# A jump past TensorE's program and back, ahead of its work, in a masked-prefix-sum and matmul kernel

## The chip, the cores and the metric

One core of a Trainium2 chip runs the kernel. The metric is the device time of one execution, in microseconds (us). For each version the median of several executions is given; a profile is one further execution, recorded by the hardware profiler.

## The reference

```python
B, S, D = 8, 8192, 512          # x: B x S x D f32, lengths: B int64, w: D x D f32
mask = (pos < lengths[:, None, None])
cs = np.cumsum(x * mask, axis=1)
midpoints = (lengths // 2).clip(0)
mid_features = cs[b_idx, midpoints, :]
return np.matmul(mid_features[:, None, :], w).squeeze(1)
```

Only one row of each running sum is used. So for each of the 8 batches the kernel adds up the first n = min(lengths // 2 + 1, lengths) rows of x, and multiplies the 8 sums by w. With the lengths of this draw n is 570, 2690, 256, 2057, 905, 3772, 3859 and 571: 14,680 rows of 2 KB.

## The kernel before

The sums are made on TensorE: a matmul of 0/1 weights (128 rows of x by 8 batches) with 128 rows of x adds those rows up into `s_ps` in PSUM, at the row of the batch that they belong to. Four such matmuls, for the four groups `j` of a tile, go to four bands of columns of the array and write four bands of `s_ps`; the bands are added at the end.

The rows of a batch come in whole blocks of 512 rows (1 MB, the tile `xt`, with 8 block slots for each of two buffers `q`) and a remainder of under 512 rows (the tile `rem`, in four pieces). The first block of batch 0 has a tile of its own, `first`, and is loaded without knowing the lengths. Batches are handled in pairs: a loop of four passes whose body holds batch `q=0` and batch `q=1`. How many blocks a batch has is known only at run time. Each engine that needs it reads the lengths into registers (the class `Counts`), and `whole_blocks` is a nest of eight branches, one for each block: the body of block k is entered if n has that many rows.

The program is written out by hand, engine by engine, with semaphores:

- SyncE (`block.sync`, line 166) issues the lengths, `first`, and the `xt` blocks, each once its slot is free (`s_free`, line 178), and at the end half of the output.
- ScalarE (`block.scalar`, line 193) issues w (line 154) ahead of everything, then the remainders, and at the end evicts and stores the other half.
- GpSimd clears `rem`. VectorE (line 259) builds the weights and, per batch, copies them to `cur` (line 322).
- TensorE (`block.tensor`, line 335) first clears `s_ps` (line 344, after VectorE's `zb`), broadcasts the row counts to all partitions (`n_ps`, line 347), reads the lengths into registers (lines 115 and 348), adds `first` (line 353), and enters the loop (line 354): wait for `cur` and `rem` (`take`, line 103), four matmuls on `rem`, then for each block a wait for its landing (again line 103) and four matmuls on `xt` (line 339), then a branch (line 145). After the loop come a small closing matmul (line 373), the sums' transposition by a `fold` matrix (line 379), and the product with w (line 387). An fp32 matmul is four instructions: a weight load and a matmul, twice.

A DMA adds 16 to its semaphore, one from each of the 16 DMA engines when its part has landed; `take(pe, s_full[q][k], 16)` therefore waits for the slowest of the sixteen.

[...]

Of the kernel before, what the change touches and what calls it, by code (L numbers as in the profile page):

```python
# [11 lines left out]
P = 128  # L12
# [3 lines left out]
def kernel(  # L16
# [17 lines left out]
    B, S, D = x.shape  # L34
    G = 4
    BLK = P * G
    NB = S // 2 // BLK
    KC = D // P
# [4 lines left out]
    PARTS = [(256, 0, 2, 4), (128, 1, 4, 4), (64, 3, 4, 2)]  # L43
# [6 lines left out]
    def sb(name, shape, dt=F32):  # L50
        return ctx.enter_context(nc.sbuf_tensor(name, shape, dt))

    def ps(name, shape):
        return ctx.enter_context(nc.psum_tensor(name, shape, F32))

    def sem(name):
        return tc.alloc_semaphore(name)

    xt = sb("xt", [P, 2, NB, G, D])
    first = sb("first", [P, G, D])  # L60
    rem = sb("rem", [P, 2, G, D])
    wt = sb("wt", [P, KC, D])
# [3 lines left out]
    n_f = sb("n_f", [1, B])  # L66
    ones = sb("ones", [1, P])
    zb = sb("zb", [1, 32], mybir.dt.bfloat16)
# [8 lines left out]
    first_w = sb("first_w", [P, B])  # L77
    table = sb("table", [P, B * (WT + 1)])
    cur = sb("cur", [P, 2, WT])
    zero = sb("zero", [1, D])  # L80
    fold_i = sb("fold_i", [P, B], I32)
    fold = sb("fold", [P, B])
    s_sb = sb("s_sb", [P, KC, P])
    mf_sb = sb("mf_sb", [P, KC, B])
    o_sb = [sb(f"o_sb{h}", [B, D // 2]) for h in range(2)]

    s_ps = ps("s_ps", [P, D])
    mf_ps = [ps(f"mf_ps{h}", [P, D]) for h in range(2)]
    o_ps = ps("o_ps", [P, D])
    n_ps = ps("n_ps", [P, D])  # L90

    s_full = [[sem(f"full{q}_{k}") for k in range(NB)] for q in range(2)]
    s_free = [[sem(f"free{q}_{k}") for k in range(NB)] for q in range(2)]
    s_rem = [sem(f"rem{q}") for q in range(2)]
    s_rfree = [sem(f"rfree{q}") for q in range(2)]
    s_cur = [sem(f"cur{q}") for q in range(2)]
    s_w, s_first, s_len1, s_go, s_out = sem("w"), sem("first"), sem("len1"), sem("go"), sem("out")
    s_pool, s_dve, s_pe = sem("pool"), sem("dve"), sem("pe")
    s_act = sem("act")

    def take(eng, s, n):

        eng.wait_ge(s, n).then_inc(s, -n)  # L103
# [39 lines left out]
    def whole_blocks(eng, n, body, k=0):  # L143
        if k < NB:
            with eng.If_cmp(n, BLK * (k + 1), "IS_GE"):
                body(k)
                whole_blocks(eng, n, body, k + 1)

    DVE_SEL, DVE_N, DVE_MASK = 2, 6, 28
# [16 lines left out]
    @block.sync  # L166
    def _(sp):
        ns = Counts(sp, s_len1, 16)
        sp.sem_inc(s_go, 1)
        base, at = sp.alloc_register("sp_base"), sp.alloc_register("sp_at")  # L170
        sp.reg_mov(base, 0)
        ns.without_first(base)
        with sp.Fori(0, B // 2):
            for q in range(2):
                n = ns.rows(q)

                def load_block(k):
                    take(sp, s_free[q][k], 1)
                    sp.dma_start(
                        out=xt[:, q, k],  # L180
                        in_=rows(sp, at, base, k * BLK, BLK).rearrange("(p g) d -> p g d", g=G),
                    ).then_inc(s_full[q][k], 16)

                whole_blocks(sp, n, load_block)

                sp.reg_alu(base, base, S, ALU.add)
                sp.reg_alu(base, base, ~(S - 1), ALU.bitwise_and)
            ns.next_pair()

        sp.wait_ge(s_dve, DVE_LAST)  # L190
        sp.dma_start(out=out[:, :D // 2], in_=o_sb[0][:]).then_inc(s_out, 16)
# [143 lines left out]
    @block.tensor  # L335
    def _(pe):
        def add(j, weights, rows):

            return pe.matmul(s_ps[32 * j:32 * j + B], lhsT=weights, rhs=rows,  # L339
                             start=False, stop=False, skip_group_check=True,  # L340
                             tile_position=(0, 32 * j))

        pe.wait_ge(s_dve, DVE_SEL)
        pe.matmul(s_ps[:], lhsT=zero[:, :P], rhs=zero[:], start=True, stop=False,  # L344
                  skip_group_check=True)
        pe.wait_ge(s_dve, DVE_N)
        pe.matmul(n_ps[:, :B], lhsT=ones[:], rhs=n_f[:], start=True, stop=True).then_inc(s_pe, 1)  # L347
        ns = Counts(pe, s_go, 1)
        ns.without_first()
        pe.wait_ge(s_dve, DVE_MASK)  # L350
        pe.wait_ge(s_first, 16)
        for j in range(G):
            add(j, first_w[:], first[:, j])
        with pe.Fori(0, B // 2):
            for q in range(2):
                take(pe, s_cur[q], 1)
                take(pe, s_rem[q], 16 * (len(PARTS) + 1))
                for j in range(G):
                    mm = add(j, cur[:, q, B + j * B:2 * B + j * B], rem[:, q, j])
                    if j == 0:  # L360
                        mm.then_inc(s_pe, 1)
                mm.then_inc(s_rfree[q], 1)

                def add_block(k):
                    take(pe, s_full[q][k], 16)
                    for j in range(G):
                        mm = add(j, cur[:, q, :B], xt[:, q, k, j])
                    mm.then_inc(s_free[q][k], 1)

                whole_blocks(pe, ns.rows(q), add_block)  # L370
            ns.next_pair()

        pe.matmul(s_ps[:32, :1], lhsT=zb[:], rhs=zb[:, :1], start=False, stop=True,  # L373
                  skip_group_check=True).then_inc(s_pe, 1)

        for h in range(2):
            pe.wait_ge(s_dve, DVE_MASK + 1 + h)
            for i in range(2):
                mm = pe.matmul(mf_ps[h][:, i * B:(i + 1) * B], lhsT=s_sb[:, 2 * h + i],  # L379
                               rhs=fold[:], start=True, stop=True)  # L380
            mm.then_inc(s_pe, 1)
        pe.wait_ge(s_w, 16)
        for kc in range(KC):
            if kc % 2 == 0:
                pe.wait_ge(s_dve, DVE_MASK + 3 + kc // 2)
            for j in range(4):
                mm = pe.matmul(o_ps[32 * j:32 * j + B, :P], lhsT=mf_sb[:, kc],  # L387
                               rhs=wt[:, kc, j * P:(j + 1) * P],
                               start=(kc == 0), stop=(kc == KC - 1), tile_position=(0, 32 * j))
            if kc % 2:  # L390
                mm.then_inc(s_pe, 1)

    block.__exit__(None, None, None)
    nc.sync.wait_ge(s_out, 32)
# [30 lines left out]
```

## Time and profile before

| | us |
|---|---|
| median of 5 executions (lowest, highest) | 89.78 (89.05, 92.21) |
| profiled execution, its own time | 90.06 |
| its span, first to last instruction | 87.9 |
| TensorE busy with matmuls / weight loads | 51.6 / 9.3 |
| VectorE, GpSimd, ScalarE busy | 8.1, 4.0, 2.0 |
| bytes moved by DMA | 31.28 MB, 356 GB/s over the span |
| mean clock granted to TensorE | 0.843 of full speed |

A row of the profile names the line, the engine and the tiles (out<-in). PE is TensorE's matmul side, PEld its weight loads, and a "q" after an engine's name is its instruction sequencer, which does waits, branches and DMA issues. DMA queue q1 is fed by SyncE and q10 by ScalarE. The rows of slices cut the span into 40 equal pieces; their digits are tenths.

### The profile page before, as it was taken

What the parts mean: (1) busy time and instruction counts of PE and PEld (TensorE: products, weight loads), DVE (VectorE), ACT (ScalarE), POOL (GpSimd) and SP (SyncE); (2) the same over time, 40 slices, a digit from 0 to 9 for tenths busy, and PEclk for the clock granted to TensorE, in tenths of its full rate; (3) what the DMA queues carried; (4) which work ended last, traced back from release to release, by engine and by line L of the source; (5) the groups of instructions that cost most, each with busy time, mean ns of one, the idle gap of its engine ahead of it and who ended that gap; (6) DMA issues with size and microseconds to landing.
All of it is one profiled execution on the core that took longest, in us unless ns stands there. A gap on an engine that the chain in (4) does not pass through costs nothing. (4 is left out here: it accounts for less than half of the span.)

```text
span 87.9 us, 1267 instructions
## 1 busy us (share of the span) xinstructions
PE 51.6 (59%) x317; PEld 9.3 (11%) x317; DVE 8.1 (9%) x42; ACT 2.0 (2%) x4; POOL 4.0 (5%) x9
## 2 busy tenths in 40 slices
PE   1801605996409795089944087754963487777720
PEld 1300000120001010001100000000210000010610
DVE  3685000000000000000000000000000000000520
ACT  0000000000000000000004200000000000000020
POOL 0970000000000000000000000000000000000000
PEclk9999999999995799755699855597599955599999
DMA  1899999999999999999999999999999999930000
GB/s 30 320 429 306 382 403 422 425 414 417 443 391 417 429 417 421 417 417 416 418 421 418 415 438 417 417 425 417 417 429 417 417 429 421 432 145 7 0 3 4
DMA packets 4693, 31.28 MB, mean 356 GB/s; under 512 B 658, under 2 KB 674, under 8 KB 946
## 3 DMA queue, kind: packets, MB, share of 16 engines
q1 hardware_dynamic: 3762, 27.27, 75.1%
q10 hardware_dynamic: 928, 3.97, 11.4%
q8 instruction: 1, 0.02, 0.1%
q14 instruction: 2, 0.02, 0.0%
HBM read 31.23 MB, written 0.02 MB: 355 GB/s over the span
## 5 line engine op out<-in xcount | busy, mean ns | idle before, releaser
L339 PE MATMUL s_ps<-xt,cur 128*8 128x512 f32 x200 | 34.5, 782 | 21.1 <-PEq L103 21.1
L339 PE MATMUL s_ps<-rem,cur 128*8 128x512 f32 x64 | 12.5, 866 | 4.9 <-PEq L103 4.7
L339 PEld LDWEIGHTS s_ps<-xt,cur 128*8 128x8 f32 x200 | 4.4, 92 | 49.3 <-issue 49.3
L322 DVE COPY cur<-table 128x40 f32<-128x40 f32 x8 | 1.4, 184 | 55.2 <-PE s_ps L339 55.2
L339 PE MATMUL s_ps<-first,first_w 128*8 128x512 f32 x8 | 1.9, 1040 | 4.3 <-DMA first<-in_x_dram 4.3
L257 POOL MEMSET rem<- 128x2048 f32 x2 | 3.5, 1805 | 0.0
L339 PEld LDWEIGHTS s_ps<-rem,cur 128*8 128x8 f32 x64 | 1.8, 98 | 16.6 <-issue 16.5
L344 PE MATMUL s_ps<-zero 1*128 1x512 f32 x2 | 2.1, 1136 | 1.8 <-DVE zb L268 1.8
L268 DVE COPY s_sb<-s_ps 128x256 f32<-128x256 f32 x2 | 0.8, 424 | 17.4 <-PE s_ps L373 17.4
L240 ACT ACT_TABLE_LOAD x1 | 1.3, 1283 | 47.4 <-issue 47.4
L379 PE MATMUL mf_ps<-fold,s_sb 128*128 128x8 f32 x8 | 1.1, 260 | 0.5 <-DVE s_sb L268 0.5
L243 ACT COPY o_sb<-o_ps 8x128 f32<-8x128 f32 x2 | 0.5, 259 | 35.4 <-PE o_ps L387 35.4
L387 PE MATMUL o_ps<-wt,mf_sb 128*8 128x128 f32 x32 | 1.1, 273 | 0.0
L379 PEld LDWEIGHTS mf_ps<-fold,s_sb 128*128 128x128 f32 x8 | 1.0, 190 | 0.6 <-DVE s_sb L268 0.6
L347 PEld LDWEIGHTS n_ps<-n_f,ones 1*128 1x128 f32 x2 | 0.7, 332 | 1.0 <-DVE n_f L268 0.5
L387 PEld LDWEIGHTS o_ps<-wt,mf_sb 128*8 128x8 f32 x32 | 0.8, 89 | 0.0
L344 PEld LDWEIGHTS s_ps<-zero 1*128 1x128 f32 x2 | 0.5, 305 | 1.8 <-DVE zb L268 1.8
L268 DVE COPY o_sb<-o_ps 8x128 f32<-8x128 f32 x2 | 0.6, 280 | 0.9 <-PE o_ps L387 0.8
L339 PEld LDWEIGHTS s_ps<-first,first_w 128*8 128x8 f32 x8 | 0.2, 90 | 4.4 <-DVE table L268 4.4
L268 DVE MEMSET zero<- 1x512 f32 x1 | 0.5, 485 | 1.1 <-SPq L48 1.1
L268 DVE TENSOR_SCALAR thr_i<-thr_i 128x2 int32<-128x2 int32 x1 | 0.5, 490 | 0.0
L347 PE MATMUL n_ps<-n_f,ones 1*128 1x8 f32 x2 | 0.4, 286 | 0.0
(36 smaller groups left out, 5.5 us busy)
## 6 DMA issues: line engine op xcount, KB each, us to landing
xt<-in_x_dram SPq DMA_DIRECT2D x25, 1024.0 KB, 15.5
rem<-in_x_dram ACTq DMA_DIRECT2D x3, 512.0 KB, 7.2
wt<-in_w_dram ACTq DMA_DIRECT2D x1, 1024.0 KB, 4.9
first<-in_x_dram SPq DMA_DIRECT2D x1, 1024.0 KB, 6.9
rem<-in_x_dram ACTq DMA_DIRECT2D x3, 256.0 KB, 6.5
rem<-in_x_dram ACTq DMA_DIRECT2D x3, 128.0 KB, 6.5
rem<-in_x_dram ACTq DMA_DIRECT2D x3, 32.0 KB, 5.5
rem<-in_x_dram ACTq DMA_DIRECT2D x1, 64.0 KB, 6.4
```

Of the source, the lines that this page charges most:

```text
L240: act.copy(out=warm[:], in_=zero[:, :1])
L243: copy = act.copy(out=o_sb[1][:, j * P:(j + 1) * P], in_=o_ps[64 + 32 * j:64 + 32 * j + B, :P])
L257: pool.memset(rem[:, q], 0.0).then_inc(s_rfree[q], 1)
L268: do(*args, **kw).then_inc(s_dve, 1)
L322: dve.tensor_copy(out=cur[:, b % 2], in_=table[:, b * WT:(b + 1) * WT]).then_inc(s_cur[b % 2], 1)
L339: return pe.matmul(s_ps[32 * j:32 * j + B], lhsT=weights, rhs=rows, start=False, stop=False, skip_group_check=True, tile_position=(0, 32 * j))
L344: pe.matmul(s_ps[:], lhsT=zero[:, :P], rhs=zero[:], start=True, stop=False, skip_group_check=True)
L347: pe.matmul(n_ps[:, :B], lhsT=ones[:], rhs=n_f[:], start=True, stop=True).then_inc(s_pe, 1)
L379: mm = pe.matmul(mf_ps[h][:, i * B:(i + 1) * B], lhsT=s_sb[:, 2 * h + i], rhs=fold[:], start=True, stop=True)
L387: mm = pe.matmul(o_ps[32 * j:32 * j + B, :P], lhsT=mf_sb[:, kc], rhs=wt[:, kc, j * P:(j + 1) * P], start=(kc == 0), stop=(kc == KC - 1), t ...
```

## The change

Everything that TensorE does is put into a loop of two passes, under a condition that holds in the second pass alone. In the first pass the branch of the condition leads from the start of the program to its end, and the loop's own branch leads back. The instructions inside are the same, in the same order. On TensorE a register move, two branches, a register step and the loop's closing branch come in; the other engines' instructions stay as they are. Lines from 344 on move down by three.

```diff
-        pe.wait_ge(s_dve, DVE_SEL)
-        pe.matmul(s_ps[:], lhsT=zero[:, :P], rhs=zero[:], start=True, stop=False,
-                  skip_group_check=True)
+
+        with pe.Fori(0, 2) as i:
+            with pe.If(i >= 1):
+                pe.wait_ge(s_dve, DVE_SEL)
+                pe.matmul(s_ps[:], lhsT=zero[:, :P], rhs=zero[:], start=True, stop=False,
+                          skip_group_check=True)
...
-        with pe.Fori(0, B // 2):
-            for q in range(2):
-                take(pe, s_cur[q], 1)
+                with pe.Fori(0, B // 2):
+                    for q in range(2):
+                        take(pe, s_cur[q], 1)
...
-        pe.wait_ge(s_w, 16)
-        for kc in range(KC):
-            if kc % 2 == 0:
-                pe.wait_ge(s_dve, DVE_MASK + 3 + kc // 2)
+                pe.wait_ge(s_w, 16)
+                for kc in range(KC):
+                    if kc % 2 == 0:
+                        pe.wait_ge(s_dve, DVE_MASK + 3 + kc // 2)
```

More of the change, by code (lines that the diff above doesn't have):

```diff
@@ L341, in add @@
                              tile_position=(0, 32 * j))
-        pe.wait_ge(s_dve, DVE_SEL)
-        pe.matmul(s_ps[:], lhsT=zero[:, :P], rhs=zero[:], start=True, stop=False,
-                  skip_group_check=True)
[L346 to L353, printed above, removed]
@@ L354, in _ @@
-        with pe.Fori(0, B // 2):
-            for q in range(2):
-                take(pe, s_cur[q], 1)
-                take(pe, s_rem[q], 16 * (len(PARTS) + 1))
-                for j in range(G):
-                    mm = add(j, cur[:, q, B + j * B:2 * B + j * B], rem[:, q, j])
-                    if j == 0:
-                        mm.then_inc(s_pe, 1)
[L362 to L381, printed above, removed]
-        pe.wait_ge(s_w, 16)
-        for kc in range(KC):
-            if kc % 2 == 0:
-                pe.wait_ge(s_dve, DVE_MASK + 3 + kc // 2)
[L386 to L391, printed above, removed]
+        with pe.Fori(0, 2) as i:
[3 more added lines that the diff above has]
+                          skip_group_check=True)
+                pe.wait_ge(s_dve, DVE_N)
+                pe.matmul(n_ps[:, :B], lhsT=ones[:], rhs=n_f[:], start=True, stop=True).then_inc(s_pe, 1)
+                ns = Counts(pe, s_go, 1)
+                ns.without_first()
+                pe.wait_ge(s_dve, DVE_MASK)
+                pe.wait_ge(s_first, 16)
+                for j in range(G):
+                    add(j, first_w[:], first[:, j])
+                with pe.Fori(0, B // 2):
+                    for q in range(2):
+                        take(pe, s_cur[q], 1)
+                        take(pe, s_rem[q], 16 * (len(PARTS) + 1))
+                        for j in range(G):
+                            mm = add(j, cur[:, q, B + j * B:2 * B + j * B], rem[:, q, j])
+                            if j == 0:
+                                mm.then_inc(s_pe, 1)
+                        mm.then_inc(s_rfree[q], 1)
+                        def add_block(k):
+                            take(pe, s_full[q][k], 16)
+                            for j in range(G):
+                                mm = add(j, cur[:, q, :B], xt[:, q, k, j])
+                            mm.then_inc(s_free[q][k], 1)
+                        whole_blocks(pe, ns.rows(q), add_block)
+                    ns.next_pair()
+                pe.matmul(s_ps[:32, :1], lhsT=zb[:], rhs=zb[:, :1], start=False, stop=True,
+                          skip_group_check=True).then_inc(s_pe, 1)
+                for h in range(2):
+                    pe.wait_ge(s_dve, DVE_MASK + 1 + h)
+                    for i in range(2):
+                        mm = pe.matmul(mf_ps[h][:, i * B:(i + 1) * B], lhsT=s_sb[:, 2 * h + i],
+                                       rhs=fold[:], start=True, stop=True)
+                    mm.then_inc(s_pe, 1)
+                pe.wait_ge(s_w, 16)
+                for kc in range(KC):
+                    if kc % 2 == 0:
+                        pe.wait_ge(s_dve, DVE_MASK + 3 + kc // 2)
+                    for j in range(4):
+                        mm = pe.matmul(o_ps[32 * j:32 * j + B, :P], lhsT=mf_sb[:, kc],
+                                       rhs=wt[:, kc, j * P:(j + 1) * P],
+                                       start=(kc == 0), stop=(kc == KC - 1), tile_position=(0, 32 * j))
+                    if kc % 2:
+                        mm.then_inc(s_pe, 1)
```

## The prediction

> **What bounds the kernel now.** I read the page's slices first, then its queues, then the stretches around the end, the order of time there, and last the queues again in short windows.
>
> ```profile
> DMA  1899999999999999999999999999999999930000
> q1 hardware_dynamic: 3762, 27.27, 75.1%
> q10 hardware_dynamic: 928, 3.97, 11.4%
> q8 instruction: 1, 0.02, 0.1%
> q14 instruction: 2, 0.02, 0.0%
> ```
>
> From about 4 us to 77 us the 16 DMA engines are full. 31.28 MB have to come in; nothing that TensorE does in that stretch is worth time by itself. The last two rows are transfers that no line of the kernel issues: the engines' own code, 16 KB each.
>
> What happens where the stream stops (columns: us, then busy time by engine, TensorE clock, DMA share, GB/s):
>
> ```profile
> 75.00:76.00 1.00, 0.42 (x4) 0.15 (x8) 0.00 (x0) 0.00 (x0) 0.00 (x0) 0.50 1.04 434
> 77.00:78.00 1.00, 0.47 (x4) 0.00 (x0) 0.00 (x0) 0.00 (x0) 0.00 (x0) 0.82 0.61 254
> 78.50:79.00 0.50, 0.50 (x12) 0.22 (x8) 0.00 (x0) 0.00 (x0) 0.00 (x0) 1.00 0.08 33
> 79.00:79.50 0.50, 0.50 (x12) 0.03 (x4) 0.00 (x0) 0.00 (x0) 0.00 (x0) 1.00 0.04 16
> 79.50:79.90 0.40, 0.40 (x8) 0.00 (x0) 0.00 (x0) 0.00 (x0) 0.00 (x0) 1.00 0.05 20
> ```
>
> One engine of 16 is a share of 0.06, and 434 / 16 = 27 GB/s. So from 78.5 us on one single DMA engine still works, and the other fifteen are done. The records of single packets say the same: the last five 8-KB packets start one after another at 78.35, 78.66, 78.96, 79.28 and 79.58 us. The landings of the last block (a DMA adds to its semaphore 16 times, one an engine) are at 77.54 for the first engine, 78.95 for the fifteenth and 80.34 for the sixteenth: the last engine is 1.39 us behind all others. TensorE waits for it:
>
> ```profile
> 78.91 1.05 PE L339 MATMUL s_ps<-rem,cur 128*8 128x512 f32 x8
> 80.44 0.15 PEld L339 LDWEIGHTS s_ps<-xt,cur 128*8 128x8 f32 x8 [1.41 <-issue]
> 80.47 1.04 PE L339 MATMUL s_ps<-xt,cur 128*8 128x512 f32 x8 [0.51 <-PEq L103]
> ```
>
> Line 103 is the wait for the block; it ends at 80.36, and from there a fixed tail of 7.5 us runs to the span's end at 87.9.
>
> Where does the straggler come from? For each block I took the gap between the fifteenth and the sixteenth landing. Blocks complete at 12.10, 15.72 and 18.13 us with gaps of 0.08, 0.08 and 0.11. The next one, at 22.05, has a gap of 1.45, and every later block keeps one between 1.39 (at the end) and 2.7. So one engine lost some 1.4 us between 18.1 and 22 us and never caught up, because each engine has its own backlog and none idles. The queues between 18 and 20 us:
>
> ```profile
> q1 hardware_dynamic: 114, 0.83, 99.7%
> q8 instruction: 1, 0.02, 3.3%
> ```
>
> 3.3% of 16 engines' 2 us is 1.06 us on one engine; the packet starts at 18.50. It is the only code transfer on q8 in the span. It starts some 0.2 us after TensorE, at 18.16 to 18.31, runs the third block of the second half of its loop body (k=2, q=1). Counting four instructions for each fp32 matmul, that is number 251 to 268 of TensorE's program[...]. [...]
>
> **The change, part by part.** (1) The jump. In pass 0 TensorE does one register move, a taken branch over the whole body, a register step, a taken branch back, and then the compare that falls through. Rows for these:
>
> ```profile
> L354 PEldq MOVE  x1: 37/37/37, 8.4 to 8.4; - x1
> L354 PEldq COMPARE_BRANCH  x4: 64/207/207, 26.8 to 81.0; - x4
> L145 PEldq COMPARE_BRANCH  x33: 64/64/377, 14.3 to 80.5; - x33
> ```
>
> 37 + 377 (the dearest taken branch) + 78 (the shortest register step, line 127) + 207 + 64 = 0.76 us, with 207 for the first branch 0.59; with gaps of some 0.06 up to 1.06. TensorE is free at 1.01 us (its start branch) and its first matmul waits for VectorE's zb until 1.79. It comes to that wait at 1.6 to 2.1, so at most 0.3 late. Behind it are the matmul for n_ps (ends at 4.08; VectorE reads it only at 6.82, 2.7 us of cover), the register load (3.38 to 4.67), and the `first` matmuls, held until 8.28 by their DMA. After these TensorE waits for rem until 14.00. Cost on the path: 0. If the jump also waits for a code load of 1.06 to 1.31 us (the packets at 18.50 and, after the span, at 89.00), it still stays under that cover.
>
> (2) The code load moves. TensorE reaches the far end at about 1.3 us and the 16 KB go out at about 1.5, if it follows as promptly as at 18.5. The data stream is not full then:
>
> ```profile
> 0.00:1.50 1.50, 0.00 (x0) 0.00 (x0) 0.38 (x1) 0.00 (x0) 0.20 (x4) 1.00 0.00 0
> 2.00:2.75 0.75, 0.75 (x1) 0.28 (x2) 0.47 (x3) 0.00 (x0) 0.44 (x4) 1.00 0.65 153
> 3.25:5.00 1.75, 0.83 (x3) 0.33 (x1) 1.19 (x10) 0.00 (x0) 1.75 (x2) 1.00 0.98 417
> 7.75:8.75 1.00, 0.36 (x4) 0.15 (x8) 0.21 (x2) 0.00 (x0) 0.00 (x0) 1.00 0.66 197
> ```
>
> Nothing before 1.9; eight engines start on wt at 2.0, the other eight at 2.35 to 2.95; and between `first` and the first xt block, 7.75 to 8.75, about half of the engines are idle again. A load from 1.5 to 2.8 fits before the late eight's first packet; on one of the early eight it would leave 0.7 us of lag, of which the second hole takes up to 0.7. And the straggler is of the late kind: at 18.13 there are eight early and eight late landings (16.73 to 17.62, 17.80 to 18.13), at 22.05 eight early, seven late and it. So I take the whole lag away: gain 1.39 us at the last landing. Bounds: 0, if the lag is kept from the start; 1.45, what it had lost by 22.05.
>
> (3) What is late next. The fifteenth engine: the last block would land at 78.95. TensorE must be ready: the block before it (now at 77.92) lands 1.4 earlier as well, at 76.5, its matmuls take 1.04 us (at half clock 1.89, as at 75.58) and those of rem 1.05, so it is through at 78.6 to 79.1. The tail of 7.5 us then starts 1.3 to 1.39 us earlier.
>
> (4) At the end pass 1 adds a register step and a branch not taken (0.14 us) before the drain of line 393, which waits for matmuls from 83.54 to 84.27 anyway: 0. [...]
>
> [...] after 18.5 the loop goes back three times, its branches cost 207 ns, and q8 carries nothing more until 89.0. [...]
>
> **The rivals.** (A) The lag only changes its place: the load goes out late (after 3 us) or is not absorbed, and its engine is last from the first block on. For: in the full stream the load cost 1.4, not 1.06. Against: the two holes above. Time 89.8 less 0 to 0.8: 89.0 to 89.8. (B) It doesn't do what it says: [...] it stays at 18.5: 89.8. Against: no row. (C) Slower: [...] two extra loads, of which the holes take one or so: +1.4, some 91.2. It decides from two q8 packets more than now. Against: the single record in four passes.
>
> **How the numbers follow.** Main case 0.66, A 0.16, B 0.08, C 0.10. The profiled execution took 90.06 (span 87.9 and 2.1 around it), 0.3% over the median of 89.78. With 1.35 (between 1.3 and 1.39) off: 88.7 for the profiled one, 88.4 against the median. The runs before spread from 89.05 to 92.21, so the main case alone is 87.9 to 89.0; reaching up through most of A and leaving out B's upper part and C, the range is 87.9 to 89.5. About 1% is what a measurement can tell here, that is 88.9: most of the main case lies below it (0.60) and a little of A (0.02): faster 0.62; A, B and the rest of the main case within 1%: 0.27; slower 0.11.
>
> **What would show it.** A q8 instruction packet before 3 us and none at 18.5; gaps between the fifteenth and sixteenth landing of 0.1 to 0.2 in every block from 20 us on; no stretch at 0.04 to 0.06 DMA share before the last landing, now near 79.0; the tail from there still 7.5 us. Wrong if: the packet is early and the 1.4-us gap stands from the first block on (A); it is still at 18.5 (B); or q8 has three or more packets (C).

## The result, and the profile after

| | before | after |
|---|---|---|
| median, us | 89.94 (79 executions) | 89.53 (42 executions) |
| lowest, highest | 88.73, 92.21 | 88.46, 90.75 |
| profiled execution, and its span | 90.06, 87.9 | 90.13, 88.2 |

The ratio of the times is 0.9946, with a 95% interval of 0.9924 to 0.9968: the change makes the kernel faster by 0.5%, 0.4 to 0.5 us. It was predicted to bring 1.35. (Ratios, here and below, leave out executions that took over 1.5% more than the fastest one of their kernel, a slower state; medians are of all executions, so the two can differ.)

The profiled execution of the changed kernel is no shorter than that of the kernel before. Its queues over the whole span (packets, MB, share of 16 engines):

```profile
q1 hardware_dynamic: 3762, 27.27, 74.7%
q10 hardware_dynamic: 928, 3.97, 11.9%
q8 instruction: 1, 0.02, 0.1%
q14 instruction: 2, 0.02, 0.0%
```

It is again one code load on q8 (a packet of 16 KB that the profile gives the kind "instruction"), as many as before, but at another time. The queues between 4 and 6 us:

```profile
q10 hardware_dynamic: 75, 0.49, 59.9%
q1 hardware_dynamic: 40, 0.33, 38.6%
q8 instruction: 1, 0.02, 2.9%
```

and between 18 and 20 us, where the kernel before had it:

```profile
q1 hardware_dynamic: 116, 0.84, 100.2%
```

So the load has moved, from 18.50 to 4.68 us, but not to 1.5 us. And 4.68 is in the full stream: q10 carries w, q1 starts on `first`. TensorE's jump itself (columns: name, count, shortest/median/longest ns, first and last start):

```profile
L345 PEldq COMPARE_BRANCH  x2: 69/212/356, 1.3 to 2.2; - x2
L145 PEldq COMPARE_BRANCH  x33: 64/69/232, 14.5 to 79.5; - x33
```

The far branch runs from 1.26 to 1.61 us and the next instruction at the far end follows 0.06 us later: no stall there. It takes 356 ns, and the branch of line 145 that took up to 377 ns in the kernel before now takes at most 232. Why these two branches are the dear ones, the traces do not show. In the kernel before the dear branch ran from 14.34 to 14.71 us, on the way to the second half of the loop body, and the load came 3.8 us later; here it comes 3.1 us after 1.61.

The stretches at the end (us, busy time by engine, TensorE clock, DMA share, GB/s):

```profile
77.00:78.00 1.00, 1.00 (x8) 0.21 (x11) 0.00 (x0) 0.00 (x0) 0.00 (x0) 0.50 0.71 295
78.00:78.50 0.50, 0.50 (x4) 0.00 (x0) 0.00 (x0) 0.00 (x0) 0.00 (x0) 0.50 0.16 66
78.50:79.00 0.50, 0.50 (x8) 0.17 (x4) 0.00 (x0) 0.00 (x0) 0.00 (x0) 0.50 0.00 0
```

Bytes are counted where a packet starts. The last packet of data starts at 78.49 us; the last landing is at 79.25 instead of 80.34. So 1.1 us were won at the landing in this pair of profiles. The order of time shows why the span did not follow:

```profile
76.93 1.90 PE L339 MATMUL s_ps<-xt,cur 128*8 128x512 f32 x8 [0.59 <-PEq L103]
78.58 1.94 PE L339 MATMUL s_ps<-rem,cur 128*8 128x512 f32 x8
80.29 1.44 PE L339 MATMUL s_ps<-xt,cur 128*8 128x512 f32 x8
```

The clock that TensorE was granted is 0.50 here until 81.1 us. The eight matmul passes on a tile take 1.90 us instead of 1.04, three such groups follow each other without a wait, and the last block starts at 80.29 though it has been there since 79.25. In the profile before, the clock was full from 77.4 us. From the last landing to the span's end it is 7.60 us there and 8.94 here. The periods of half clock come at other times in other profiles, so this pair alone tells neither the size of the gain nor what it was lost to. That needed more profiles.

### The profile page after: what moved, and what is told of

Read it like the earlier page. It is cut to its first block, busy times and chain, and to the rows that moved or that the text cites. A ratio compares the mean times of both kernels' runs of the same rounds, so it can differ in the third digit from the quotient of the medians.

```text
span 88.2 us, 1276 instructions
## 1 busy us (share of the span) xinstructions
PE 49.9 (57%) x317; PEld 9.3 (10%) x317; DVE 8.1 (9%) x42; ACT 2.0 (2%) x4; POOL 4.0 (5%) x9
## 5 line engine op out<-in xcount | busy, mean ns | idle before, releaser
L339 PE MATMUL s_ps<-xt,cur 128*8 128x512 f32 x200 | 33.7, 764 | 22.9 <-PEq L103 22.8
L339 PE MATMUL s_ps<-rem,cur 128*8 128x512 f32 x64 | 11.6, 805 | 3.5 <-PEq L103 3.5
```

## The experiments

Two theories stood beside each other. **L**: one DMA engine lags by what the code load costs it, and the time follows the last landing; where the load falls decides what is left of the lag. **C**: the landing gains its full 1.1 to 1.4 us each time, and TensorE's half clock takes it back.

**The two kernels again.** Unchanged, for a second profile each; no edit.

> The kernel before, unchanged, for a second profile. If the 1.4-us lag of one DMA engine is a property of the code load (theory L), the load starts near 18.5 us again, 3.5 to 4 us after TensorE's first branch into the second half of the loop, and every block from 22 us on has a gap of 1.2 to 1.6 us or more between its fifteenth and sixteenth landing. If the lag was chance (rival), the gap is below 0.8 us at the end although the load is there.

> The changed kernel, unchanged, for a second profile. Theory L: load at 4.5 to 5 us, gap of some 0.4 us between the last two landings of each block at the end, last landing near 79.2 us. Theory C (TensorE's clock takes the gain back): the time from the last landing to the end of the span is 7.5 us where TensorE has the full clock from 77 to 82 us and up to 9 us where it has half. Rival (a wait of TensorE's after the landing that the change brought, the same in each profile): near 9 us again at full clock.

The kernel before: load at 18.49 us, lag (sixteenth landing after the fifteenth, in the last block) 1.01 us, last landing 80.06. The lag comes again with the load, a little smaller than expected. The changed kernel: load at 4.89, lag 0.30, last landing 79.72, and here the clock is full from 76.4 us:

```profile
78.25 1.05 PE L339 MATMUL s_ps<-rem,cur 128*8 128x512 f32 x8
79.83 0.14 PEld L339 LDWEIGHTS s_ps<-xt,cur 128*8 128x8 f32 x8 [1.46 <-issue]
79.86 1.04 PE L339 MATMUL s_ps<-xt,cur 128*8 128x512 f32 x8 [0.56 <-PEq L103]
```

With full clock TensorE waits for the last block again, and from the last landing to the end it is 7.64 us. So the change itself adds nothing behind the landing. What is new is that the landing is at 79.72, later than the 79.25 of the first profile by as much as the whole measured gain.

**The jump, but late.**

```diff
+        pe.wait_ge(s_first, 16)
         with pe.Fori(0, 2) as i:
```

> The changed kernel, but TensorE waits for the tile first (about 8.3 us) before it jumps, so that the load, some 3 to 4 us later, comes at 11.5 to 12.5 us, in the full data stream and behind the hole at 7.75 to 8.75. Theory L: its engine lags 1.0 to 1.5 us in every block from 14 us to the end, as in the kernel before, and the time is that of the kernel before, ratio 0.997 to 1.003, at most 0.5 us more for the later weights. Rival (the jump itself, not its place, brings the gain): gap of 0.4 us and ratio 0.993 to 0.996.

The load came at 12.39 us, the lag is 1.38 us to the end, the last landing at 80.10, and the ratio 0.9992 (0.9955 to 1.0028). The stretches of this kernel around the last packets:

```profile
78.50:79.00 0.50, 0.50 (x8) 0.16 (x4) 0.00 (x0) 0.00 (x0) 0.00 (x0) 0.50 0.04 16
79.00:79.50 0.50, 0.50 (x8) 0.03 (x3) 0.00 (x0) 0.00 (x0) 0.00 (x0) 0.50 0.08 33
79.50:80.00 0.50, 0.50 (x8) 0.13 (x4) 0.00 (x0) 0.00 (x0) 0.00 (x0) 0.50 0.00 0
```

One engine alone at a share of 0.04 to 0.08, as in the kernel before. The same jump brings nothing that can be told from zero when its load falls into the full stream. This speaks against the rival that the jump itself helps. By the ratios alone it would not be settled, since this interval and the changed kernel's overlap a little; the lag decides.

**The jump behind TensorE's set-up.** The clearing, `n_ps`, the register load and `without_first` stand ahead of the two-pass loop:

```diff
+        ns = Counts(pe, s_go, 1)
+        ns.without_first()
         with pe.Fori(0, 2) as i:
             with pe.If(i >= 1):
-                ns = Counts(pe, s_go, 1)
-                ns.without_first()
```

> The changed kernel, but TensorE does its set-up (clearing, row counts, register load) before the jump, which then comes at about 5.1 us, and the load at 8.0 to 9.0 us, where about half of the DMA engines have a hole before the first xt block. Theory L: if the loaded engine has the hole, its lag at the end is 0.5 us or less, like the changed kernel or better, ratio 0.990 to 0.996; if the load comes after the hole it is 1.0 to 1.4 us and the ratio 0.997 to 1.003. Rival (lag by chance): no relation of lag and place.

The far branch ended at 5.79, the load came at 9.48 us, so behind the hole and not in it: lag 1.50 us, last landing 80.40, ratio 0.9989 (0.9945 to 1.0032). The place was missed, but the second case of theory L came out.

**TensorE's program cut down, and padded again.** The cut-down kernel leaves out most of the matmuls, as its expectation says, so its sums are incomplete and only its times count. That the load would stay away in a shorter program and come back with the padding was an estimate of mine. The padding is never run:

```diff
                 whole_blocks(pe, ns.rows(q), add_block)
+                if q == 0:
+                    with pe.If_cmp(ns.regs[0], 1 << 20, "IS_GE"):
+                        for _ in range(50):
+                            add(0, first_w[:], first[:, 0])
```

The third kernel has this padding and the changed kernel's two-pass loop.

> From the kernel before, TensorE's program is cut [...]: one matmul of four on each block, two of four on each remainder, one of four with first and with w, seven block slots instead of eight (three quarters of the sums are left out; the same bytes are loaded). TensorE is then never the bound. Theory L: no q8 load between 1 and 80 us, the last two landings of the last block within 0.3 us, last landing near 79.0 us, and time 1.0 to 2.0 us under the kernel before. Rival (one DMA engine is slow by itself): gap of 1 us or more without any load.

> As l1_small, with 200 instructions that never run between the two halves of the loop body[...]. Theory L: a load on q8 3 to 4 us after the first branch over the padding (at 18 to 19 us), gap of 1.0 to 1.5 us to the end, time 0.8 to 1.4 us over l1_small. Rival: equal to l1_small within 0.3 us.

> As l2_small_padded, with the jump past the program and back of the changed kernel. Theory L: load at 4.5 to 5 us, gap 0.2 to 0.5 us, time 0.5 to 1.1 us under l2_small_padded. Theory C (TensorE's clock takes half of the gain back in the full kernel): here, where TensorE is never the bound, the gain is clearly larger than the 0.4 to 0.7 us between the two full kernels, 0.9 us or more. If it is 0.5 to 0.7 here as well, the clock takes nothing on average and the landing itself gained only that.

The cut-down program's queues from 14 to 80 us have no code load at all:

```profile
q1 hardware_dynamic: 3334, 24.17, 88.2%
q10 hardware_dynamic: 668, 2.62, 9.8%
```

Its last two landings are 0.08 us apart, the last is at 79.08, and the ratio to the kernel before is 0.9904 (0.9870 to 0.9938). It has no dear branch on TensorE either; with the padding there is one, over the padding. The row of the cut-down kernel, then that of the padding's branch:

```profile
L145 PEldq COMPARE_BRANCH  x31: 64/64/237, 14.7 to 79.3; - x31
L372 PEldq COMPARE_BRANCH  x4: 201/208/342, 15.5 to 78.9; - x4
```

With these 200 instructions that nobody runs, the queues from 18 to 21 us show

```profile
q8 instruction: 1, 0.02, 2.2%
```

at 19.28 us, and the lag is 1.29 us to the end, the last landing 81.15, the ratio 0.9993 (0.9953 to 1.0033): about 0.9% over the kernel without padding, with intervals that don't meet, and medians 90.22 against 89.22. This shows the cost of the load most directly, with the same bytes of data, and a rival falls with it: an engine that is slow by itself would lag without a load too, and there the lag was 0.08. Of the 2.07 us between the two last landings 1.21 are the lag; the other 0.86 are the other fifteen engines, which are later too (78.99 and 79.85). With the jump on top the load is at 4.65, the lag 0.02 (0.2 to 0.5 was expected), the last landing 79.38 and the ratio 0.9949 (0.9913 to 0.9986); the median of 89.13 is that of the kernel without padding again. On theory C the three are inconclusive. The medians of the padded pair lie 1.1 us apart, their ratios only 0.4%, with intervals that overlap. And the premise did not hold: even with a quarter of the matmuls TensorE was bound at the end where it had half clock (cut-down kernel: eight matmul passes from 76.8 to 81.6 us, 8.84 us from landing to end).

**The jump between the row counts and the register load.**

```diff
         pe.matmul(n_ps[:, :B], lhsT=ones[:], rhs=n_f[:], start=True, stop=True).then_inc(s_pe, 1)
+        with pe.Fori(0, 2) as i:
+            with pe.If(i >= 1):
                 ns = Counts(pe, s_go, 1)
```

> The changed kernel with the jump behind the clearing and the row counts, but ahead of the register load, so that TensorE enters the far end near 3.9 us and the load comes at 7.0 to 7.7 us and runs into the hole at 7.75 to 8.75 us. Theory L: the lag is used up in the hole, gap at the end 0.1 to 0.4 us, last landing 78.9 to 79.5 us, ratio to the kernel before 0.988 to 0.995; if the loaded engine is one that has no hole, gap 0.9 us or more and ratio 0.997 to 1.003.

> The jump ahead of the register load (as e5_mid_jump), timed once more beside the other two, for a second profile. Theory L: load at 6.8 to 7.2 us, lag below 0.2 us at the end, ratio 0.988 to 0.996, equal to or up to 0.4 us under the changed kernel. If its lag is 0.9 us or more here, the place of the load relative to the hole is a matter of chance.

In two profiles the load came at 6.88 and 7.02 us, and the lag at the end was 0.03 and 0.10 us: the hole after `first` (7.75 to 8.75 us, a DMA share of 0.66 in the kernel before) took nearly all of it. Stretches of the first of the two:

```profile
78.00:78.50 0.50, 0.50 (x8) 0.12 (x4) 0.00 (x0) 0.00 (x0) 0.00 (x0) 1.00 0.32 131
78.50:79.00 0.50, 0.50 (x8) 0.00 (x0) 0.00 (x0) 0.00 (x0) 0.00 (x0) 1.00 0.35 147
79.00:79.50 0.50, 0.23 (x4) 0.00 (x0) 0.00 (x0) 0.00 (x0) 0.00 (x0) 1.00 0.01 0
```

The engines stop together, up to 79 us several at once. Yet the last landings are 79.62 and 79.67, later than expected in the first run and not at 78.95, and the ratios 0.9983 (0.9942 to 1.0025) and 0.9928 (0.9891 to 0.9966). So without a straggler the other engines are later than they were (79.60 and 79.57 us, against 78.46 to 79.05). The two ratios of one kernel differ by as much as the change brings, so whether this place is better than that of the changed kernel can't be told.

**Both kernels once more, timed on one chip.**

> The kernel before against itself, timed, for the width of the measurement and a third profile. Ratio 0.997 to 1.003 with an interval of about 0.004 on both sides. Theory L: lag 1.0 to 1.5 us at the end, last landing 79.9 to 80.5 us. Theory C: time from the last landing to the end of the span 7.5 to 7.7 us at full clock from 78 us on, 8.3 to 9.0 us at half clock there.

> The changed kernel, timed once more beside the kernel before, and a third profile. Theory L with the lag partly kept: lag 0.3 to 0.5 us, last landing 79.2 to 79.8 us, so 0.5 to 1.0 us ahead of the kernel before, and a ratio of 0.989 to 0.996. If the landing gains its full 1.1 to 1.4 us in this pair and the time does not (ratio 0.995 or more), theory C stands: the clock takes it back.

Before against itself: 0.9977 (0.9942 to 1.0011), load at 18.12, lag 0.97, last landing 79.43, earlier than the 79.9 to 80.5 expected. After: 0.9950 (0.9916 to 0.9983), load at 4.78, lag 0.37, last landing 79.68. The gain in time came again; in this pair of profiles the landing gained nothing, so theory C's test, a full gain at the landing without one in time, was not met.

**A wait ahead of that jump.**

```diff
+        pe.wait_ge(s_dve, 11)
         with pe.Fori(0, 2) as i:
```

> As e5_mid_jump, with TensorE waiting for VectorE's 11th step (3.87 us) before it jumps, so that it enters the far end near 4.5 us and the load comes at 7.6 to 8.2 us, after the engine's part of the tile first and in the hole. Theory L with the issue delay: SyncE's issues of the first five blocks are then not held up (each 0.33 to 0.37 us, as in the kernel before), the bytes moved by 20 us are 6.88 MB or more, the lag at the end is 0.1 to 0.4 us, last landing 78.8 to 79.4 us, ratio 0.987 to 0.994. If the load is too late for the hole: lag 1.0 us or more, ratio 0.997 to 1.003. If an issue is still held up by 0.4 us or more, 6.70 to 6.85 MB by 20 us and a ratio like the changed kernel's, 0.993 to 0.997.

Load at 8.21 us, lag 0.51, last landing 79.47, ratio 0.9938 (0.9905 to 0.9972), median 89.16. SyncE's issues were not held up, as expected, but the lag is larger than expected and the bytes by 20 us are 6.83 MB, under the 6.88 that were asked for. It is as fast as the changed kernel; that it is faster can't be told.

**What the profiles say together.** All from the landing and packet records; "MB" is data alone, with packets under way counted in part; "other engines" is the fifteenth landing of the last block, "held" the longest of SyncE's first five `xt` issues.

| kernel | load at | lag at the end | other engines | last landing | held, ns | MB by 20 us |
|---|---|---|---|---|---|---|
| before, 3 profiles | 18.50, 18.49, 18.12 | 1.39, 1.01, 0.97 | 78.95, 79.05, 78.46 | 80.34, 80.06, 79.43 | 368, 369, 368 | 6.89, 6.90, 7.06 |
| late jump | 12.39 | 1.38 | 78.73 | 80.10 | 368 | 6.87 |
| behind set-up | 9.48 | 1.50 | 78.90 | 80.40 | 368 | 6.86 |
| wait, then jump | 8.21 | 0.51 | 78.96 | 79.47 | 368 | 6.83 |
| before register load, 2 | 6.88, 7.02 | 0.03, 0.10 | 79.60, 79.57 | 79.62, 79.67 | 860, 1019 | 6.77, 6.74 |
| after, 3 profiles | 4.68, 4.89, 4.78 | 0.43, 0.30, 0.37 | 78.82, 79.42, 79.31 | 79.25, 79.72, 79.68 | 807, 1024, 916 | 6.90, 6.79, 6.77 |

In the means of three, the lag falls from 1.12 to 0.37 us (0.76 won) and the other engines end at 79.18 instead of 78.82 (0.36 given back). That leaves 0.39 us at the last landing, close to the measured 0.4 to 0.5. The agreement can be chance: the last landings of the kernel before alone lie 0.9 us apart. Theory C is not excluded by it either. Two of the three profiles after still have half clock at the last landing and none of the three before, so the spans did not shorten at all (87.57 before, 87.97 after, in the mean). What the half clock takes over many executions stays open.

Where the 0.36 us come from is shown in part. SyncE's issue of a block takes 0.33 to 0.37 us; with the load at 4.7 to 7.0 us one of the first five is held up, in one profile two. The five in the first profile of the kernel before:

```profile
L179 SPq DMA_DIRECT2D xt<-in_x_dram x5: 333/333/368, 5.0 to 8.5; - x5
```

and in the second profile of the changed one:

```profile
L179 SPq DMA_DIRECT2D xt<-in_x_dram x5: 332/368/1024, 5.0 to 9.8; - x5
```

What a held issue waits for, the traces do not show. The fifth issue starts at 9.8 us here instead of at 8.5. In four of the five profiles with such a hold 6.74 to 6.79 MB are in by 20 us, against 6.89 to 7.06 before; 0.13 MB at the stream's 421 GB/s is 0.3 us. But the first profile of the changed kernel has a hold and no deficit, and the kernel with the wait has a small deficit and no hold. The padded kernel without the jump also had a hold (1192 ns, 6.70 MB, other engines at 79.85), though no load had come yet; with the jump it was 801 ns, 6.85 MB and 79.35. Over all fourteen profiles the other engines end at 78.82 to 79.85 in the seven with a hold of 0.8 us or more (mean 79.42) and at 78.46 to 79.05 in the seven without (mean 78.86). That a hold goes with a later end is therefore shown as a tendency. That it is the cause, and that the early load causes the hold, is likely, but neither is shown apart from the rest.

## Why the prediction was right or wrong

- **What bounds the kernel** was right: one engine, behind the others by what a code load costs it, sets the last landing, and where TensorE has its full clock that landing sets the end. The padded kernel shows the lag, 1.29 us against 0.08, with only the padding added.
- **The direction, and the jump's cost on the path** were right. The sequencer came to its first matmul at 2.35 us, 0.56 late and not at most 0.3 as I had worked out (two more register moves, and gaps of 0.06 to 0.15 us), and nothing waited for it: VectorE reads `n_ps` at 6.82 as before.
- **The time of the load was the step that failed**: "the 16 KB go out at about 1.5, if it follows as promptly as at 18.5". I took the instruction that ran just before 18.50 for the trigger; that coming to the far end of the program would start the load was an estimate from this one place. What goes with the load everywhere is one dear branch of TensorE, of 342 to 382 ns, where the other taken branches after the start take 201 to 237: in all thirteen profiles with a load the packet follows the end of that branch by 3.0 to 3.8 us, and the one profile without a dear branch has no load. The row with its 377 ns was in my own working; I used it as a price and did not ask which branch it was. At these delays a jump at 1.06 us, where TensorE comes to its own program, can't bring the load ahead of the data, which start at 1.98. The packet came at 4.68 to 4.89 us, into transfers that were under way, and 0.30 to 0.43 us of lag was left where I had taken all of it away. So case A, the lag in part only moved, came true in part: in the first profile the gap between the last two landings is 1.94 us for w, 1.35 for `first`, 0.53 for the first `xt` block, and 0.43 at the end. The hole did what I had written of it.
- **What is late next was mis-sized**: the fifteenth engine was taken to stay at 78.95. It moved from 78.82 to 79.18 on average, which took back about half of what the lag had won.
- **The 1.39 us were one profile's.** The mean of three is 1.12. I had made the sum with the largest.
- **The fixed tail of 7.5 us** is fixed at full clock alone (7.50 to 7.64 us). In the fourteen profiles it is 7.50 to 8.96 us.
- The measured 89.53 lies just above the range's end of 89.5 and inside case A's 89.0 to 89.8; I had given case A 0.16, because I held the hole and the early packet for enough.
- Rival B fell: the load moves with the jump, from 18.50 to 4.68 us. Rival C fell too: no profile has more than one q8 load before its last landing; its two extra loads were an estimate. What each load brings is not known: the second packet of the kernel before, behind its span (at 89.00, 88.78 and 88.13 us), is in no profile with the jump. In going by the single record in four passes I was right: the next instruction came 0.06 us after the far branch, and q8 carried one load.

## What to carry to other kernels

In this stream, which keeps all DMA engines full (a share of 1.01 to 1.02 from 10 to 75 us), a packet of 16 KB that one engine alone had to carry was paid at the end, however early it came, unless the stream had a hole behind it, as the loads at 9.5 and 12.4 us (lag 1.50 and 1.38) and those at 6.9 and 7.0 (0.03 and 0.10) show; the gap between the last two landings of a transfer shows it. Before moving such a thing, find its trigger and its delay from more than one place in the trace, and look whether an engine that issues transfers is held up meanwhile (0.8 to 1.0 us here, in the five profiles with the load at 4.7 to 7.0). A single profile of each side can mislead: the same pair of kernels showed 1.1 us at the last landing or none at all, and where the periods of half clock fell moved the end by up to another 1.3 us.

## What the hardware showed that was not expected

- A code load of 16 KB comes 3.0 to 3.8 us after the end of one dear branch of TensorE of 342 to 382 ns (13 profiles), takes 0.92 to 1.07 us as a packet, and costs its engine 1.0 to 1.5 us in a full stream (0.97 to 1.50 in six profiles).
- 200 instructions that never run cost 1 us of median (89.22 to 90.22), and bring a code load with them (at 19.28 us); one DMA engine is then 1.29 us behind the others at the end.
- From the last landing to the end of the span it is 7.50 to 7.64 us in six profiles where TensorE has full clock from 79 us or earlier, and 8.43 to 8.96 in seven with half clock until 80.7 us or later (8.10 in one where half clock begins again at 84.2). In the first profile of the changed kernel, one of the seven, TensorE began on the last block 1.0 us after it had landed, so an earlier landing would not have helped it in full.
